# Adaptive products kept out of the first seam of a two-layer decoder trunk, and the openings behind the other seams in three passes over half a PSUM bank

## The chip, the cores and the metric

The kernel runs on one core of one Trainium2 chip. The metric is the device time of one execution in microseconds (us); the profile is one further execution with the hardware profiler on.

## What is computed

Two layers on 256 tokens of width 2048, batch 1, in float32. In both, every sub-layer is a root-mean-square norm, a shift and a scale that depend on a condition vector `c`, the sub-layer, and a residual add with a gate that depends on `c` too.

```python
cond = silu(c)
for i in range(2):
    sh1, sc1, g1, sh2, sc2, g2 = split(cond @ ada_w[i] + ada_b[i], 6)   # the adaptive columns
    h = rmsnorm(x, norm_mix[i]) * (1 + sc1) + sh1
    y = attn_pool_mixer(h) if i == 0 else ssd_mixer(h)
    x = x + g1 * y
    h = rmsnorm(x, norm_ffn[i]) * (1 + sc2) + sh2
    x = x + g2 * (square(relu(h @ ffn_w1[i])) @ ffn_w2[i])              # hidden width 8192
return rmsnorm(x, final_norm)
```

The mixer of layer 0 is windowed attention in three head groups beside a pooling branch; that of layer 1 is a chunked state-space scan (Mamba-2).

## The kernel before, in words

**GEMMs.** Tokens and weights are split into a high part in the `fp32r` format and a low part, the remainder, so a product takes three terms: high by high, high by low, low by high. `split` (lines 163 to 168) makes the parts of a weight tile: ScalarE copies the high part (166), VectorE subtracts (167). Weight tiles `raw` of 1 MB come through SP's DMA queue into a ring of four; each is split in two halves into rings of four `hi` and four `lo` tiles. An activation tile `h(kt)` has 512 columns: 256 tokens high, then 256 low. `mm` (194 to 203) forms the terms in one of two ways. With `one` it makes three passes of 256 columns that all add into half a PSUM bank. Otherwise the first pass streams high and low tokens together, 512 columns, and the second adds the low weight into the second half of the bank; the two halves are joined later by `evac` (303 to 306): a ScalarE copy and a VectorE add. Each pass has a weight load of its own. Tiles that go through `mm` with `one` start 64 bytes after an aligned address (`SHIFT`).

**Adaptive columns.** Each of 192 jobs (`ada_tile`, 83 to 87) loads a 1 MB tile of `ada_w` into the same `raw` ring, multiplies it with the condition on VectorE and sums along the row (line 86). `Feed.tick`, called after each weight load, runs jobs at an even rate: `Feed(jobs, slots)` spreads them over so many loads. The 36 jobs that mixer 0 gets are the first gate and 20 of the 32 that the norm before the first MLP needs; the other 12 run in `up_wide` (474 to 494), one per k-tile.

**Seams.** Where one sub-layer ends and the next begins, the residual is gated (`gated`, lines 445 and 446), squared and summed (315), the root is taken on GpSimd (337), the row is scaled (370, 372), turned on TensorE (393) and modulated. At the first seam (mixer 0 to MLP 0) `turn_out` copies the turned blocks to `xr`: blocks 0 and 2 on VectorE (403), 1 and 3 on ScalarE (401). `up_wide` then makes `h` from them (408 to 416) and runs a GEMM over all of PSUM with row tiles `w1w`. At the other two seams, into mixer 1 and into MLP 1, `opening` runs the first GEMM (three output tiles beside the 64 time-step columns, and four output tiles). For k-tiles 0 to 7 it goes over the first 128 tokens, then over the other 128 (`mm_chunk`, lines 209 and 210), while the rest of the input is still being turned; for k-tiles 8 to 15 it takes both at once (245, 246). Its weights come from a `Stream`.

**Order.** The Tile framework plans the order of each engine's instructions when the kernel is built, by priorities and a model of their costs; on the chip each engine runs its list in that order, and so does SP's DMA queue.

Of the kernel before, what the change touches and what calls it, by code (L numbers as in the profile page):

```python
# [8 lines left out]
F32 = mybir.dt.float32  # L9
F32R = mybir.dt.float32r  # L10
AF = mybir.ActivationFunctionType
# [27 lines left out]
def trunk(ctx, tc, xin, cb, fin, adaT, par, m0, m1, tri_in, icnt, pw_in,  # L39
# [130 lines left out]
    class Stream:  # L170
# [5 lines left out]
        def half(self, i):  # L176
            while len(self.halves) <= i:
                n = len(self.halves)
                ap, nk = self.aps[n // 2]
                if n % 2 == 0:  # L180
                    self.raw = wp.tile([P, D], F32, name="raw")
                    SP.dma_start(self.raw[:, 0:nk * self.width], ap)
                size = nk // 2 * self.width
                self.halves.append(split(wp, self.raw[:, (n % 2) * size:(n % 2 + 1) * size], nk // 2))
                if n % 2:
                    feed[0].tick()
            return self.halves[i]
# [16 lines left out]

    def mm_chunk(acc, hi, lo, r, c, first, last):

        def part(ap):
            return ap.rearrange("p (s c t) -> p s c t", s=2, c=2)[:, :, c, :]
        PE.matmul(part(acc), hi, part(r), start=first and c == 0, stop=False, skip_group_check=True)
        PE.matmul(acc[:, T + c * P:T + (c + 1) * P], lo, r[:, c * P:(c + 1) * P], start=False, stop=last, skip_group_check=True)  # L210

    def opening(h, stream, nt, extra=None):


        acc = [accp.tile([P, 512], F32, name="acc") for _ in range(nt)]

        def tiles(kt):
            hi, lo, n = stream.half(kt // 2)
            for t in range(nt):
                ts = slice(t * P, (t + 1) * P)  # L220
                yield acc[t], hi[:, kt % 2, ts], lo[:, kt % 2, ts], h(kt)

        for kt in range(8):
            if kt == 2:
                h.piece_of(1, 0)
            if kt == 6:
                h.piece_of(0, 1)
            for a, hi, lo, r in tiles(kt):
                mm_chunk(a, hi, lo, r, 0, kt == 0, False)
        if extra:  # L230
            extra = extra()
        for kt in range(8):
            if kt == 1:
                h.piece_of(1, 1)
            if kt in (2, 4, 6):
                stream.half(3 + kt // 2)
            if kt in (2, 6):
                h.piece(2 + kt // 4)
            for a, hi, lo, r in tiles(kt):
                mm_chunk(a, hi, lo, r, 1, False, False)  # L240
            if extra:
                extra(kt)
        for kt in range(8, KT):
            for a, hi, lo, r in tiles(kt):
                PE.matmul(a, hi, r, start=False, stop=False, skip_group_check=True)
                PE.matmul(a[:, T:2 * T], lo, r[:, 0:T], start=False, stop=(kt == KT - 1), skip_group_check=True)
            if extra:
                extra(kt)
        return acc
# [49 lines left out]

    def chunks(ap, n=4):  # L300
        return [(ap[c], n) for c in range(ap.shape[0])]

    def evac(ps, dst, parts=P):
        corr = tp.tile([P, T], F32, name="corr", bufs=1)
        S.activation(corr[0:parts], ps[0:parts, T:2 * T], AF.Copy)
        V.tensor_tensor(dst, ps[0:parts, 0:T], corr[0:parts], op=ALU.add)


    ssq = [None, None]
# [30 lines left out]
    class Hidden:  # L340
# [55 lines left out]
        def turn_out(self, i, c):  # L396
            ps = self.turned_of(i, c, i % 2 == 0)
            dst = self.xr[:, i * 4:(i + 1) * 4, c * P:(c + 1) * P]
            src = ps.rearrange("p (k t) -> p k t", k=4)
            if i % 2:  # L400
                S.activation(dst, src, AF.Copy)
            else:
                V.tensor_copy(dst, src)

        def affine(self, kt):
            return mod[self.l][self.a][:, kt:kt + 1], mod[self.l][self.b][:, kt:kt + 1]
# [67 lines left out]
    def up_wide(h, jobs):  # L474
# [5 lines left out]
        with tc.tile_pool(name="sweep1", bufs=4) as fp:  # L480
            acc = [accp.tile([P, 512], F32, name="acc") for _ in range(5)] + [misc.tile([P, 512], F32, name="mp") for _ in range(3)]
            for kt in range(KT):
                for half in range(2):
                    if half == 0:
                        h.make(kt, h.xr[:, kt, :])
                    elif jobs:
                        ada_run(jobs.pop(0))
                    hi, lo, _ = load_row(w1w[kt, :, half * 1024:(half + 1) * 1024], fp)
                    for j in range(8):
                        n = half * 8 + j  # L490
# [5 lines left out]
    def mlp(l, h, nx, wide=()):  # L496
# [3 lines left out]
        with tc.tile_pool(name=f"mlp{l}", bufs=2) as mp:  # L500
# [7 lines left out]
            def new_z():  # L508
                return mp.tile([P, T], F32, name="z", bufs=3)
# [8 lines left out]
            def up(q, b, first=False):  # L518
                acc = opening(h, h.stream, 4) if first else gemm_ws(chunks(w1[l, q * 4 + b]), h, 512, one=True)
                ht = new_hid(q, b)  # L520
                for t in range(4):
                    z = new_z()
                    if first:
                        evac(acc[t], z)
                    squared_relu(z if first else acc[t], z, ht, t)

            def down(q, b):
                def done(acc, c):
# [50 lines left out]
    def mixer0(ctx0, jobs2, following):  # L579
# [54 lines left out]
        with tc.tile_pool(name="mix0", bufs=2) as mp:  # L634
# [64 lines left out]
                S.activation(cat_a[sl, pr, 0:T], o[sl, 0:T], AF.Copy)  # L699
                V.tensor_tensor(cat_a[sl, pr, T:2 * T], o[sl, 0:T], cat_a[sl, pr, 0:T].bitcast(F32), op=ALU.subtract)  # L700

            feed[0] = Feed(jobs2, 31)
            tiles = []
            for b in range(6):
                if b:
# [65 lines left out]
    def mixer1(h, nx):  # L771
        with tc.tile_pool(name="mix1", bufs=2) as mp:
# [54 lines left out]
            def conv_silu(ps, ch, dst):  # L827
                xp = mp.tile([P, 3 + T], F32, name="xp")
                G.memset(xp[:, 0:3], 0.0)
                if ps.shape[1] == T:  # L830
                    S.activation(xp[:, 3:], ps, AF.Copy)
                else:
                    evac(ps, xp[:, 3:])
                cv = mp.tile([P, T], F32, name="cv")
                S.activation(cv, xp[:, 0:T], AF.Identity, bias=pcol(C_CB + ch), scale=pcol(C_CW + ch))
                for j in range(1, 4):
# [271 lines left out]
```

## Time and profile before

| | |
|---|---|
| median of three executions | 2560.23 us (2559.2 to 2566.05) |
| the profiled execution | 2565.11 us, span 2563.3 us from the first to the last instruction |
| TensorE passes | 2480.7 us busy, 97%, 15752 passes |
| weight loads on TensorE | 2217.8 us busy, 87% |
| VectorE | 1855.4 us busy, 72% |
| ScalarE | 1301.8 us busy, 51% |
| adaptive products (line 86) | 192, 2288 ns each |
| transfers | 664 MB, 259 GB/s on average |

TensorE's share is so high that a stage is read by where TensorE waits, for whom, and at which clock it runs. A pass is a MATMUL row, PE in the views; a weight load is a LDWEIGHTS row, PEld. VectorE is DVE, ScalarE ACT, GpSimd POOL, and SPq is SP's DMA queue. Durations of passes overlap, since they are pipelined: the pace is read from start to start.

### The profile page before, as it was taken

How to read it: one execution, taken by the hardware profiler on the slowest of the kernel's cores; microseconds unless marked ns; L12 is line 12 of the kernel's file. 1: busy time of each engine (PE TensorE's matmuls, PEld its weight loads, DVE VectorE, ACT ScalarE, POOL GpSimd, SP SyncE). 2: the span in 40 equal slices, each digit the busy share in tenths (PEclk: the TensorE clock that was granted, in tenths of full speed). 3: DMA queues.
4: the chain of work that ended last, by engine and by line, in shares of the span. 5: the costliest groups of instructions: out<-in, count | busy, mean ns of one | idle time of the engine just before them, and what ended most of it. 6: DMA issues, size and time to landing. Idle time of an engine off the chain costs nothing.

```text
span 2563.3 us, 39160 instructions
## 1 busy us (share of the span) xinstructions
PE 2480.7 (97%) x15752; PEld 2217.8 (87%) x15752; DVE 1855.4 (72%) x2432; ACT 1301.8 (51%) x1927; POOL 18.1 (1%) x76
## 2 busy tenths in 40 slices
PE   6899989999999999999999999999999999999998
PEld 5589879989889899888888878888898998998996
DVE  7977798667777886778887888776776655456555
ACT  4355546644435445457664654664554453453453
POOL 0000000000000000000000000000000000000000
PEclk9999999999999999999999999999999999999999
DMA  9988898688887887746677777655567765555553
GB/s 392 417 341 311 299 334 291 249 305 325 309 327 292 299 316 293 268 165 233 242 276 255 244 258 251 205 187 185 191 249 277 265 245 197 185 193 192 186 189 124
DMA packets 117830, 664.02 MB, mean 259 GB/s; under 512 B 11664, under 2 KB 28432, under 8 KB 49424
## 3 DMA queue, kind: packets, MB, share of 16 engines
q1 hardware_dynamic: 117440, 661.42, 71.2%
q8 instruction: 123, 2.02, 0.3%
q14 instruction: 59, 0.48, 0.1%
q10 hardware_dynamic: 208, 0.10, 0.0%
HBM read 659.28 MB, written 2.20 MB: 258 GB/s over the span
## 4 chain that ended last, share of the span: by engine, by line
PE 82%; DVE 8%; DMA 5%; ACT 2%; issue 2%; POOL 0%; SPq 0%; ACTq 0%; DVEq 0%; POOLq 0%
PE acc L275 13%; PE acc L276 13%; PE acc L274 13%; PE acc L200 12%; PE acc L198 12%; PE acc L199 12%; DMA raw<-in_adaT_dram 5%; DVE lo L167 3%; DVE raw L86 2%; PE mp L903 1%; DVE cv L837 1%; ACT hi L166 1%; PE mp L697 0%; PE mp L393 0%; PE mp L199 0%
## 5 line engine op out<-in xcount | busy, mean ns | idle before, releaser
L166 ACT ACTIVATE hi<-raw 128x1024 fp32r<-128x1024 f32 (+1 forms) x800 | 818.5, 1026 | 962.1 <-PE acc L276 539.5
L167 DVE TENSOR_TENSOR lo<-raw,hi 128x1024 fp32r<-128x1024 f32 (+1 forms) x800 | 935.6, 1179 | 490.3 <-ACT hi L166 487.6
L200 PE MATMUL acc<-h,lo 128*128 128x256 f32 x2992 | 836.4, 281 | 7.3 <-DVE lo L167 7.1
L198 PE MATMUL acc<-h,hi 128*128 128x256 f32 x2992 | 839.1, 281 | 1.4 <-DVE dt_v L783 0.8
L199 PE MATMUL acc<-h,hi 128*128 128x256 f32 x2992 | 839.3, 281 | 0.0
L199 PEld LDWEIGHTS acc<-h,hi 128*128 128x128 f32 x2992 | 569.7, 190 | 2.2 <-issue 1.7
L200 PEld LDWEIGHTS acc<-h,lo 128*128 128x128 f32 x2992 | 561.3, 188 | 10.9 <-DVE lo L167 9.2
L198 PEld LDWEIGHTS acc<-h,hi 128*128 128x128 f32 x2992 | 564.2, 189 | 6.9 <-issue 4.3
L86 DVE SCALAR_TENSOR_TENSOR raw<-raw,cond 128x2048 f32<-128x2048 f32 x192 | 439.2, 2288 | 99.7 <-DMA raw<-in_adaT_dram 99.3
L274 PE MATMUL acc<-hi,hid 128*128 128x512 f32 x1024 | 398.6, 389 | 0.0
L275 PE MATMUL acc<-lo,hid 128*128 128x512 f32 x1024 | 398.4, 389 | 0.0
L276 PE MATMUL acc<-hi,hid 128*128 128x512 f32 x1024 | 398.3, 389 | 0.0
L274 PEld LDWEIGHTS acc<-hi,hid 128*128 128x128 f32 x1024 | 192.2, 188 | 39.9
L276 PEld LDWEIGHTS acc<-hi,hid 128*128 128x128 f32 x1024 | 192.2, 188 | 39.9
L275 PEld LDWEIGHTS acc<-lo,hid 128*128 128x128 f32 x1024 | 192.2, 188 | 39.5
L275 PE MATMUL acc<-lo,h 128*128 128x512 f32 x288 | 114.4, 397 | 2.3 <-DVE lo L167 2.3
L276 PE MATMUL acc<-hi,h 128*128 128x512 f32 x288 | 116.5, 405 | 0.0
L274 PE MATMUL acc<-hi,h 128*128 128x512 f32 x288 | 113.9, 397 | 0.3 <-ACT hi L166 0.3
L166 ACT ACTIVATE hi<-rawh 128x1024 fp32r<-128x1024 f32 x64 | 60.7, 949 | 97.2 <-DMA rawh<-in_wvq_dram 60.5
L275 PE MATMUL acc<-lo,yn 128*128 128x512 f32 x224 | 87.6, 391 | 0.0
L274 PE MATMUL acc<-hi,yn 128*128 128x512 f32 x224 | 87.5, 391 | 0.0
L276 PE MATMUL acc<-hi,yn 128*128 128x512 f32 x224 | 87.4, 390 | 0.0
(230 smaller groups left out, 2342.3 us busy)
## 6 DMA issues: line engine op xcount, KB each, us to landing
raw<-in_w_dram SPq DMA_DIRECT2D x240, 1024.0 KB, 5.0
raw<-in_adaT_dram SPq DMA_DIRECT2D x192, 1024.0 KB, 6.6
raw<-in_sx_dram SPq DMA_DIRECT2D x64, 768.0 KB, 4.3
raw<-in_sz_dram SPq DMA_DIRECT2D x32, 1024.0 KB, 5.0
raw<-in_swo_dram SPq DMA_DIRECT2D x32, 1024.0 KB, 4.9
raw<-in_wqk_dram SPq DMA_DIRECT2D x20, 1024.0 KB, 6.9
rawh<-in_wvq_dram SPq DMA_DIRECT2D x32, 512.0 KB, 12.2
rawh<-in_w1w_dram SPq DMA_DIRECT2D x32, 512.0 KB, 6.3
```

The costliest lines, as they stand in the source:

```text
L86: V.scalar_tensor_tensor(raw, raw, 1.0, cond, op0=ALU.mult, op1=ALU.mult, accum_out=acc_ada[l][:, i * KT + kt:i * KT + kt + 1])
L166: S.activation(hi, src, AF.Copy)
L167: V.tensor_tensor(lo, src, hi.bitcast(F32), op=ALU.subtract)
L198: PE.matmul(acc, hi, r[:, 0:T], start=first, stop=False, skip_group_check=skip)
L199: PE.matmul(acc, hi, r[:, T:2 * T], start=False, stop=False, skip_group_check=skip)
L200: PE.matmul(acc, lo, r[:, 0:T], start=False, stop=last, skip_group_check=skip)
L274: PE.matmul(acc[c], ah, hi, start=first, stop=False)
L275: PE.matmul(acc[c], ah, lo, start=False, stop=False)
L276: PE.matmul(acc[c], al, hi, start=False, stop=last)
L837: V.scalar_tensor_tensor(cv, xp[:, j:j + T], pcol(C_CW + j * 48 + ch), cv, op0=ALU.mult, op1=ALU.add)
L903: PE.matmul(ps[:, i * 64:(i + 1) * 64], em[c][:, i, :], xdt[c][:, i * 64:(i + 1) * 64], start=True, stop=True)
```

## The change

Four edits. The feed of mixer 0 spreads its 36 jobs over 26 weight loads in place of 31. `turn_out` remembers its last VectorE copy, and the twelve products in `up_wide` are put behind that copy on VectorE (`issue_after` adds an order of issue for the instructions on that copy's engine, and no wait for another engine). `mm_chunk` and the second part of `opening` make three passes into half a bank, where they made two over the whole; the streamed weight tiles start 64 bytes further on. So `evac` goes, and its users read PSUM directly. The time-step columns keep their two passes and their whole bank.

```diff
@@ class Stream, half
-                self.halves.append(split(wp, self.raw[:, (n % 2) * size:(n % 2 + 1) * size], nk // 2))
+                self.halves.append(split(wp, self.raw[:, (n % 2) * size:(n % 2 + 1) * size], nk // 2, SHIFT))
@@ mm_chunk
-        def part(ap):
-            return ap.rearrange("p (s c t) -> p s c t", s=2, c=2)[:, :, c, :]
-        PE.matmul(part(acc), hi, part(r), start=first and c == 0, stop=False, skip_group_check=True)
-        PE.matmul(acc[:, T + c * P:T + (c + 1) * P], lo, r[:, c * P:(c + 1) * P], start=False, stop=last, skip_group_check=True)
+        rh, rl = r[:, c * P:(c + 1) * P], r[:, T + c * P:T + (c + 1) * P]
+        out = acc[:, c * P:(c + 1) * P]
+        PE.matmul(out, hi, rh, start=first and c == 0, stop=False, skip_group_check=True)
+        PE.matmul(out, hi, rl, start=False, stop=False, skip_group_check=True)
+        PE.matmul(out, lo, rh, start=False, stop=last, skip_group_check=True)
@@ opening
-        acc = [accp.tile([P, 512], F32, name="acc") for _ in range(nt)]
+        acc = [accp.tile([P, 512], F32, name="acc")[:, 0:T] for _ in range(nt)]
...
-                PE.matmul(a, hi, r, start=False, stop=False, skip_group_check=True)
-                PE.matmul(a[:, T:2 * T], lo, r[:, 0:T], start=False, stop=(kt == KT - 1), skip_group_check=True)
+                mm(a, hi, lo, r, False, kt == KT - 1, True, True)
@@ evac
-    def evac(ps, dst, parts=P):
-        corr = tp.tile([P, T], F32, name="corr", bufs=1)
-        S.activation(corr[0:parts], ps[0:parts, T:2 * T], AF.Copy)
-        V.tensor_tensor(dst, ps[0:parts, 0:T], corr[0:parts], op=ALU.add)
@@ turn_out
-                V.tensor_copy(dst, src)
+                self.turned_last = V.tensor_copy(dst, src)
@@ up_wide
-                        ada_run(jobs.pop(0))
+                        with tc.issue_after(h.turned_last.ins):
+                            ada_run(jobs.pop(0))
@@ mlp, up
-                    z = new_z()
-                    if first:
-                        evac(acc[t], z)
-                    squared_relu(z if first else acc[t], z, ht, t)
+                    squared_relu(acc[t], new_z(), ht, t)
@@ mixer0
-            feed[0] = Feed(jobs2, 31)
+            feed[0] = Feed(jobs2, 26)
@@ mixer1, conv_silu
-                if ps.shape[1] == T:
-                    S.activation(xp[:, 3:], ps, AF.Copy)
-                else:
-                    evac(ps, xp[:, 3:])
+                S.activation(xp[:, 3:], ps, AF.Copy)
```

## Rows read from the trace of the kernel before

**Rows 1.** Stretches: start:end, length; busy PE, PEld, DVE, ACT, POOL; clock; DMA; GB/s

```profile
141.00:340.00 199.00, 196.52 (x1481) 178.30 (x1480) 157.69 (x238) 107.74 (x174) 0.25 (x4) 0.99 0.84 312
352.00:372.00 20.00, 17.35 (x77) 13.78 (x75) 19.96 (x30) 8.90 (x15) 0.00 (x0) 1.00 0.94 354
372.00:395.00 23.00, 13.93 (x55) 11.57 (x55) 20.96 (x35) 11.42 (x19) 1.27 (x2) 0.65 0.91 343
395.00:480.00 85.00, 85.00 (x721) 85.00 (x720) 63.18 (x79) 45.65 (x60) 0.00 (x0) 1.00 0.80 286
```

**Rows 2.** TensorE's passes in order of time at the first seam; start, length (us)

```profile
372.29 0.79 PE L275 MATMUL acc<-lo,cat_p 128*128 128x512 f32 x1 [2.93 <-DVE lo L167]
...
378.34 0.39 PE L275 MATMUL acc<-lo,cat_p 128*128 128x512 f32 x1
378.57 0.39 PE L276 MATMUL acc<-hi,cat_p 128*128 128x512 f32 x1
385.29 1.12 PE L393 MATMUL mp<-ident,xr 128*128 128x128 f32 x4 [6.34 <-ACT xr L370]
...
394.98 1.18 PE L198 MATMUL acc<-h,hi 128*128 128x256 f32 x5
```

**Rows 3.** VectorE in order of time there: products of line 86, last copy

```profile
367.12 2.29 DVE L86 SCALAR_TENSOR_TENSOR raw<-raw,cond 128x2048 f32<-128x2048 f32 x1
...
374.49 2.28 DVE L86 SCALAR_TENSOR_TENSOR raw<-raw,cond 128x2048 f32<-128x2048 f32 x1
...
387.91 2.28 DVE L86 SCALAR_TENSOR_TENSOR raw<-raw,cond 128x2048 f32<-128x2048 f32 x1
...
394.51 0.69 DVE L403 COPY xr<-mp 128x512 f32<-128x512 f32 x1 [1.47 <-PE mp L393]
```

**Rows 4.** Loads (PEld) and passes (PE) of the opening of MLP 1

```profile
1835.27 0.19 PEld L209 LDWEIGHTS acc<-h,hi 128*128 128x128 f32 x1
1835.32 0.33 PE L209 MATMUL acc<-h,hi 128*128 128x256 f32 x1
...
1835.49 0.22 PE L210 MATMUL acc<-h,lo 128*128 128x128 f32 x1
...
1835.55 0.33 PE L209 MATMUL acc<-h,hi 128*128 128x256 f32 x1
...
1836.65 0.19 PEld L209 LDWEIGHTS acc<-h,hi 128*128 128x128 f32 x1
```

**Rows 5.** Loads of the opening of mixer 1 at the half clock

```profile
1112.87 0.33 PEld L210 LDWEIGHTS acc<-h,lo 128*128 128x128 f32 x1
...
1113.72 0.33 PEld L210 LDWEIGHTS acc<-h,lo 128*128 128x128 f32 x1
```

**Rows 6.** Loads of a GEMM in three passes of 256 columns, in MLP 0

```profile
600.02 0.19 PEld L200 LDWEIGHTS acc<-h,lo 128*128 128x128 f32 x1
...
601.44 0.19 PEld L200 LDWEIGHTS acc<-h,lo 128*128 128x128 f32 x1
```

**Rows 7.** The chain of waits: 64-column passes of mixer 1, start, length

```profile
1184.15 3.52 PE mp L903 x32
```

**Rows 8.** SP's DMA queue in the attention stage; weight loads and job loads

```profile
251.31 0.33 SPq L157 DMA_DIRECT2D raw<-in_wqk_dram  x1
...
256.63 0.33 SPq L157 DMA_DIRECT2D raw<-in_wqk_dram  x1
258.84 6.51 SPq L85 DMA_DIRECT2D raw<-in_adaT_dram  x2
267.35 0.33 SPq L157 DMA_DIRECT2D raw<-in_wqk_dram  x1
```

**Rows 9.** Busy time by stretch, the two openings; columns as in rows 1

```profile
1109.80:1129.60 19.80, 18.60 (x137) 17.11 (x138) 19.07 (x48) 11.78 (x31) 0.60 (x3) 0.91 0.52 176
1835.00:1856.10 21.10, 19.33 (x152) 19.07 (x153) 20.17 (x48) 12.84 (x29) 0.62 (x1) 0.92 0.42 145
```

**Rows 10.** TensorE's waits behind the opening of mixer 1: us, times, longest

```profile
PE acc L198 <- DVE dt_v L783: 0.8, 1, 0.8
```

## The prediction

> **What bounds the kernel now.** I read the stretches first. From 141 to 340 us, the attention stage, TensorE is busy 196.5 of 199 us while VectorE is busy 158 [rows 1]: passes set the pace and the VectorE work lies under them. In the next two stretches, the end of the output projection and the seam to the MLP, this turns round: VectorE is busy 19.96 of 20 us and 20.96 of 23, and TensorE idles 2.65 and 9.07 us, 11.7 together, at a granted clock of 0.65 in the second [rows 1]. After 395 us the wide first GEMM has TensorE busy without a gap and VectorE 63 of 85 us [rows 1].
>
> Then TensorE's order of time in that seam. At 372.29 it had waited 2.93 us for the low half of a weight tile (line 167); the next 23 starts take 6.28 us, 0.27 each, where the last two are 0.23 apart; from the last, 378.57, to the first pass of the MLP, 394.98, are 16.4 us, most of it waits for the scaled and turned input [rows 2]. VectorE's order says what stood in front: the adaptive products of line 86, 2.2 to 2.3 us each. One starts at 367.12, just before the late low half; three more start from 374.49 to 387.91, and the copy out of PSUM that ends the turning comes at 394.51 [rows 3].
>
> Last the two openings (mixer 1 and MLP 1). In the first chunks each k-tile and output tile take a weight load and a pass for the high part, then both for the low part. The loads follow each other evenly: from 1835.27 to 1836.65 there are 12 steps, 0.115 us each, whether the pass beside them has 256 or 128 columns [rows 4]. At the half clock it is the same even step, 0.85 us for 4, 0.21 each [rows 5]. Where each load has a pass of 256 columns the step is 1.42 us for 12, 0.118 [rows 6]. Even 32 passes of only 64 columns, each with its load, need 3.52 us, 0.110 each [rows 7]. So a pass with a load of 128 columns costs about 0.115 us however few columns it streams, and the chunk passes are bound by loads, two per step, 0.230.
>
> **The first part: products moved out of the seam.** The feed of 36 jobs ends after 26 loads in place of 31, so 36 x 26/31 = 30 are out by load 26 now and six more must go into the attention stage. Of the twelve jobs of the wide GEMM three run in front of the last turned copy now [rows 3]; all twelve are to run behind it.
> (a) The late low half: the two products in front of it are gone. 2.9 us of wait, and 23 x (0.27 - 0.23) = 1.0 us of half clock behind the wait [rows 2]: 3.9.
> (b) Three products that stand in VectorE's queue on the way to 394.51, 2.2 us each from start to start: 6.6 [rows 3].
> (c) Against it, the MLP's first passes now start just as the clock comes back (0.65 in that stretch [rows 1]); earlier they may run some us at the half clock. A short stretch of it cost 1.0 in (a); I take 1.0.
> Seam: 3.9 + 6.6 - 1.0 = 9.5 gained. Bounds: 5, if other VectorE work (splits of the first weights, gating) slides into the freed places; 14, all 11.7 us of idle and what the half clock costs the passes and turnings of the second stretch, some 2.3 more.
> (d) The six jobs that move: 6 x 2.2 = 13 us of VectorE under passes that leave it 41 us free [rows 1], and 6 MB more through SP's queue and the four-slot ring of raw tiles that weights and jobs share. That ring is the cost. Two weight loads with one job between them are issued 5.3 us apart (251.31, 256.63); with two jobs between them the next comes 10.7 us later (267.35) [rows 8]. Ten of 26 loads get two jobs instead of four. The splits run some tiles ahead, and head work of attention lies between the GEMMs, so most of it is hidden; without this cover six such gaps are 6 x 5.4 = 32 us. I take 1.0, with 0 and 6 as ends, since TensorE shows no loss where the pattern occurs now.
> (e) The held products meet a GEMM with 22 us of VectorE to spare [rows 1]; SP issues their transfers in order and a fifth waits for the first product, with the next rows of weights behind it, but several k-tiles are split or loaded by then. 0; if the cover fails, the 6.6 of (b) come back.
>
> **The second part: three passes over half a bank.** Each of the 16 chunks (8 k-tiles, 2 halves of the tokens) of 3 + 4 output tiles goes from two loads and passes to three: 112 times 0.345 in place of 0.230, that is 112 x 0.115 = 12.9 us more on TensorE. For the k-tiles 8 to 15 the columns stay 768, each load beside 256 of them, 0.118 each [rows 6]: 0, at most 0.5. The shift of the streamed tiles by 64 bytes changes no instruction count: 0. Cover: TensorE idles 1.20 and 1.77 us in the two stretches, VectorE being busy nearly throughout [rows 9]; longer passes fill these 3.0. The granted clock there is 0.91 and 0.92 [rows 9], some 3.5 us lost; with fewer waits I let a third of it go, 1.2. So 12.9 - 3.0 - 1.2 = 8.7 lost. Bounds: 6.4 (all of the half clock gone) to 13.4 (nothing covered).
> The copies and adds that joined the two halves of a bank go: they lie beside passes, but the next GEMM waited 0.8 us for the last accumulator to come free after the opening of mixer 1 [rows 10]. 0.8 gained; bounds 0 (that wait belongs to the time-step columns, which keep their bank) and 1.
>
> The Trainium skill, "TensorE: Matmul & The Clock Gate", section Back-to-back issue gap, speaks of about 81 ns per pass in a stream of load and pass pairs at 128 columns. By it three passes are 0.243 against 0.230 and this part costs 112 x 0.013 = 1.5 us; no row here shows a pair under 0.110.
>
> **Sum.** -9.5 + 1.0 + 8.7 - 0.8 = -0.6 us on the profiled execution's 2565.1 (span 2563.3), which lies 4.9 us above the median of the three runs, 2560.23. On that median 2559.6: no change. About 0.3%, 7.7 us, is what a measurement of this kernel tells from none.
>
> **Rivals.** *All of the seam comes back* (0.12). All 11.7 us of idle vanish, attention hides the moved jobs, and the openings come to their lower bound because their waits and the half clock go: -14 + 6.4 - 1.0 = -8.6, 2551.6. For it: VectorE alone fills that seam. Against it: gating, squares, the power on GpSimd, scaling and turning remain a chain without any product.
>
> *Short passes are not bound by loads* (0.06). In the opening the 256-column pass lies 0.17 us before the next and the 128-column one 0.06 [rows 4]; read so, the strided pass is slow and three plain ones cost 0.174: 112 x 0.056 = 6.3 gained, half of it in front of waits, so -9.5 + 1.0 - 3.1 - 0.8 = -12.4, 2547.8. The even load steps and rows 7 speak against it. By 0.243 a triple it is -9.5 + 1.0 + 1.5 - 0.8 = -7.8, 2552.4; that is the time by the skill's section named above.
>
> *The clock falls in the chunk passes* (0.12), the one that ends slower. A chunk pass will stream 128 columns beside each load, where two loads have 384 now; in the two openings the clock has already been down for part of the time [rows 9], each time after waits and turning. At the half clock a triple costs 0.64 [rows 5] in place of 0.345. It decides from (7.7 + 0.6)/0.30 = 28 of the 112 triples on; with 60 of them at half clock +18 - 0.6, 2577. For it: streams with transposes between. Against it: the 64-column block of rows 7 ran at its full step.
>
> *The ring starves attention* (0.05): (d) beyond its end, above 9.3 us of the 32; at 12, 2570.6.
>
> *The products stay in the seam* (0.05), since the planner of the order places them by its own clock: only (a) comes, -3.9 + 1.0 + 8.7 - 0.8 = +5.0, 2565.2, no change by the bound.
>
> **How the numbers follow.** The forecast has 0.60. Within 0.3%: 0.60 + 0.05 = 0.65. Faster: 0.12 + 0.06 = 0.18. Slower: 0.12 + 0.05 = 0.17. The range takes the bounds of (a) to (d) and of the second part against each other, which seldom all fall on one side: 2551 to 2568; it leaves out the stronger half of each tail.
>
> **What would show it.** In the profile after: no line 86 between about 335 us and the last copy of line 403; the wait of 2.9 us gone; the first MLP pass 9 to 10 us earlier relative to the end of the attention stage, and that stage not over 1 us longer. In the openings three loads per step, evenly 0.115 us apart, and each opening 3 to 5 us longer. I am wrong if the loads follow at less than 0.1 us, if the clock in the openings falls under 0.85, or if the attention stage grows by more than 6 us.

## The result, and the profile after

The changed kernel takes 2577.69 us in the median (four executions, 2577.35 to 2581.04), the kernel before 2563.11 beside it (2559.2 to 2566.05): 14.6 us more, a ratio of 1.0061 with a 95% interval of 1.0041 to 1.0080. A second comparison on another chip gave 1.0053 (1.0037 to 1.0070). So it is slower by about 0.55%; the forecast was no change, and the range ended at 2568. The profiled execution took 2577.81 us, span 2576.0.

Its stretches, with the columns of [rows 1] (attention, the pooling stage and start of the projection, the first seam, the chunk passes of the openings of mixer 1 and MLP 1):

```profile
141.00:340.00 199.00, 194.05 (x1458) 174.95 (x1457) 157.47 (x238) 101.78 (x168) 0.25 (x4) 0.99 0.83 316
340.00:360.00 20.00, 14.73 (x57) 11.10 (x56) 18.35 (x33) 7.65 (x10) 0.00 (x0) 0.91 0.91 350
372.00:395.00 23.00, 18.56 (x82) 14.88 (x81) 15.38 (x23) 11.39 (x19) 1.28 (x2) 0.89 0.61 213
1112.90:1142.90 30.00, 29.73 (x185) 28.33 (x184) 23.12 (x54) 14.10 (x33) 0.69 (x3) 0.72 0.39 135
1847.70:1871.90 24.20, 24.18 (x217) 24.02 (x216) 21.66 (x51) 13.54 (x30) 0.62 (x1) 1.00 0.36 128
```

Attention left TensorE 2.5 us idle in [rows 1]; here it is 5.0. A gap of 5.3 us between 340 and 360 is new; there the kernel before had

```profile
340.00:360.00 20.00, 20.00 (x88) 16.18 (x87) 19.20 (x32) 8.23 (x14) 0.00 (x0) 1.00 0.88 306
```

The two chunk stretches, 19.8 and 21.1 us in [rows 9], are 30.0 and 24.2, and in the first the granted clock is 0.72. TensorE in order of time from the projection to the wide GEMM, as in [rows 2]:

```profile
340.97 0.50 PE L275 MATMUL acc<-lo,cat_a 128*128 128x512 f32 x1 [0.22 <-DVE lo L167]
...
352.34 1.16 PE L727 MATMUL mp<-dif,pw 128*128 128x256 f32 x2 [5.05 <-DVE dif L725]
...
386.96 0.39 PE L276 MATMUL acc<-hi,cat_p 128*128 128x512 f32 x1
389.77 0.96 PE L388 MATMUL mp<-ident,xr 128*128 128x128 f32 x4 [2.42 <-ACT xr L365]
392.75 4.96 PE L388 MATMUL mp<-ident,xr 128*128 128x128 f32 x24 [2.02 <-DVE xr L367]
...
398.38 0.85 PE L198 MATMUL acc<-h,hi 128*128 128x256 f32 x5
...
401.04 0.39 PE L199 MATMUL acc<-h,hi 128*128 128x256 f32 x1 [1.29 <-DVE h L410]
```

The wait of 2.93 us for the late low half is gone, and from the last projection pass to the first MLP pass are 11.4 us, not 16.4. But the projection ends at 386.96, not 378.57: among other things a wait of 5.05 us for the last pooled difference has come up inside it. VectorE says what stood there, and what follows the last turned copy:

```profile
345.35 2.28 DVE L86 SCALAR_TENSOR_TENSOR raw<-raw,cond 128x2048 f32<-128x2048 f32 x1
...
348.36 2.28 DVE L86 SCALAR_TENSOR_TENSOR raw<-raw,cond 128x2048 f32<-128x2048 f32 x1
...
352.11 0.18 DVE L725 TENSOR_TENSOR dif<-fix,win 128x16 f32<-128x16 f32 x1
...
397.75 0.69 DVE L398 COPY xr<-mp 128x512 f32<-128x512 f32 x1
398.36 2.28 DVE L86 SCALAR_TENSOR_TENSOR raw<-raw,cond 128x2048 f32<-128x2048 f32 x1
400.57 0.08 DVE L86 DVE_READ_ACCUMULATOR raw<-raw,cond 128x1 f32 x1
400.57 0.42 DVE L410 TENSOR_TENSOR h<-hf,h 128x256 fp32r<-128x256 f32 x1
```

No product lies between 350.6 and 398.4, as the change wants; the first one behind the copy stands in front of the first low half of `h` (line 410), which is the 1.29 us above. SP's queue shows where the projection's loads went: the first is issued at 320.03, in the kernel before at 304.04.

```profile
311.88 6.15 SPq L85 DMA_DIRECT2D raw<-in_adaT_dram  x2
320.03 0.33 SPq L157 DMA_DIRECT2D raw<-in_wo_dram  x1
```

Weight loads in the two openings, mixer 1 first:

```profile
1114.83 0.19 PEld L210 LDWEIGHTS acc<-h,hi 128*128 128x128 f32 x1
1114.94 0.19 PEld L211 LDWEIGHTS acc<-h,lo 128*128 128x128 f32 x1
1115.05 0.19 PEld L209 LDWEIGHTS acc<-h,hi 128*128 128x128 f32 x1
...
1115.68 0.19 PEld L209 LDWEIGHTS acc<-h,hi 128*128 128x128 f32 x1 [0.21 <-ACT h L431]
1116.21 0.19 PEld L210 LDWEIGHTS acc<-h,hi 128*128 128x128 f32 x1 [0.35 <-DVE h L432]
...
1118.02 0.33 PEld L210 LDWEIGHTS acc<-h,hi 128*128 128x128 f32 x1
1118.23 0.33 PEld L211 LDWEIGHTS acc<-h,lo 128*128 128x128 f32 x1
1118.44 0.33 PEld L209 LDWEIGHTS acc<-h,hi 128*128 128x128 f32 x1
1118.65 0.33 PEld L210 LDWEIGHTS acc<-h,hi 128*128 128x128 f32 x1
...
1850.19 0.19 PEld L211 LDWEIGHTS acc<-h,lo 128*128 128x128 f32 x1
1850.30 0.19 PEld L209 LDWEIGHTS acc<-h,hi 128*128 128x128 f32 x1
...
1851.41 0.19 PEld L210 LDWEIGHTS acc<-h,hi 128*128 128x128 f32 x1
```

Three even loads a step, 0.111 us each (1850.30 to 1851.41 are ten). In mixer 1 the granted clock went to its lower level, 1.2 GHz, at 1117.0, behind transposes and two waits of 0.21 and 0.35 us, and stayed there for 17.1 us: 0.21 us a load, 0.63 a step (1118.02 to 1118.65). In MLP 1 no wait breaks the chunk passes, and the granted clock stays at 2.4 GHz (1.00 in the stretch above).

### The profile page after: what moved, and what is told of

It reads as the page before. It is cut to its first block, busy times and chain, and to the rows that moved or that the text cites. A ratio compares the mean times of both kernels' runs of the same rounds, so it can differ in the third digit from the quotient of the medians.

```text
span 2576.0 us, 39484 instructions
## 1 busy us (share of the span) xinstructions
PE 2491.7 (97%) x15920; PEld 2229.5 (87%) x15920; DVE 1852.6 (72%) x2425; ACT 1304.1 (51%) x1925; POOL 23.2 (1%) x76
## 4 chain that ended last, share of the span: by engine, by line
PE 80%; DVE 7%; DMA 7%; ACT 3%; issue 2%; POOL 0%; SPq 0%; ACTq 0%; DVEq 0%; POOLq 0%
PE acc L276 12%; PE acc L275 12%; PE acc L274 12%; PE acc L200 12%; PE acc L199 12%; PE acc L198 12%; DMA raw<-in_adaT_dram 6%; DVE lo L167 2%; DVE raw L86 2%; ACT hi L166 1%; PE mp L894 1%; DVE cv L828 1%; PE acc L210 1%; DMA rawh<-in_w1w_dram 1%; PE acc L211 1%
## 5 line engine op out<-in xcount | busy, mean ns | idle before, releaser
L200 PE MATMUL acc<-h,lo 128*128 128x256 f32 x3048 | 849.2, 281 | 5.5 <-DVE lo L167 5.4
L199 PE MATMUL acc<-h,hi 128*128 128x256 f32 x3048 | 853.0, 281 | 1.3 <-DVE h L410 1.3
L198 PE MATMUL acc<-h,hi 128*128 128x256 f32 x3048 | 853.3, 281 | 0.8 <-ACT hi L166 0.8
L199 PEld LDWEIGHTS acc<-h,hi 128*128 128x128 f32 x3048 | 580.6, 191 | 4.3 <-issue 2.4
L198 PEld LDWEIGHTS acc<-h,hi 128*128 128x128 f32 x3048 | 575.3, 189 | 7.2 <-issue 3.7
L200 PEld LDWEIGHTS acc<-h,lo 128*128 128x128 f32 x3048 | 572.1, 189 | 9.8 <-DVE lo L167 7.5
L276 PE MATMUL acc<-hi,hid 128*128 128x512 f32 x1024 | 398.4, 389 | 0.0
```

The source lines that it names most:

```text
L198: PE.matmul(acc, hi, r[:, 0:T], start=first, stop=False, skip_group_check=skip)
L199: PE.matmul(acc, hi, r[:, T:2 * T], start=False, stop=False, skip_group_check=skip)
L200: PE.matmul(acc, lo, r[:, 0:T], start=False, stop=last, skip_group_check=skip)
L276: PE.matmul(acc[c], al, hi, start=False, stop=last)
```

## The experiments

Each ratio is to the kernel before on the same chip; it compares means, so it is not always the quotient of the two medians. 0.0010 is 2.6 us. The kernels with half products and half transfers, and the kernel before again, have a profile only. The second table is read from the traces. A: first projection load issued, first and last projection pass, and first pass of MLP 0, all in us after attention's first score pass. Seam: from the last projection pass to the first of MLP 0. Chunks: from first to last chunk pass of each opening, and the time of it at the lower clock level.

| kernel | median | before beside it | ratio | 95% interval |
|---|---|---|---|---|
| changed, again | 2579.65 | 2568.16 | 1.0053 | 1.0037 to 1.0070 |
| products alone (36 over 26, and hold) | 2568.57 | 2566.27 | 1.0009 | 0.9999 to 1.0018 |
| openings alone | 2573.24 | 2566.27 | 1.0025 | 1.0015 to 1.0035 |
| 36 over 26 alone | 2571.20 | 2566.27 | 1.0019 | 1.0010 to 1.0029 |
| hold alone | 2566.26 | 2566.27 | 0.9995 | 0.9985 to 1.0006 |
| products alone, pooling first | 2579.14 | 2568.16 | 1.0053 | 1.0035 to 1.0070 |
| opening of MLP 1 alone | 2569.89 | 2568.16 | 1.0013 | 0.9999 to 1.0026 |
| opening of mixer 1 alone | 2577.70 | 2565.74 | 1.0038 | 1.0024 to 1.0053 |
| third load in both openings | 2579.14 | 2567.36 | 1.0047 | 1.0032 to 1.0063 |
| changed, 36 over 31 | 2571.95 | 2567.36 | 1.0021 | 1.0010 to 1.0032 |
| two jobs moved, hold | 2562.00 | 2567.36 | 0.9982 | 0.9971 to 0.9994 |
| two jobs moved, products late | 2559.75 | 2567.36 | 0.9972 | 0.9962 to 0.9981 |
| the same with a short pass | 2566.36 | 2565.74 | 0.9999 | 0.9983 to 1.0014 |

```
kernel                      A: load  first  last   MLP 0  seam | chunks mixer 1, MLP 1 (lower clock)
before                        159.2  183.1  233.7  250.1  16.4 | 19.3 (3.4)   21.0 (3.4)
before, again                 160.8  185.1  235.8  252.0  16.2 | 18.9 (0)     21.0 (3.4)
changed                       174.3  188.5  241.3  252.7  11.4 | 29.9 (17.1)  24.1 (0)
changed, again                174.9  189.1  243.0  254.7  11.7 | 28.0 (6.8)   24.1 (0)
products alone                174.5  188.6  242.6  254.3  11.7 | 18.9 (0)     21.0 (3.4)
36 over 26 alone              176.2  190.3  243.4  256.9  13.6 | 18.9 (0)     21.0 (3.4)
hold alone                    158.7  183.0  233.5  247.0  13.5 | 18.9 (0)     19.4 (0)
pooling first                 176.8  191.0  245.3  257.0  11.7 | 18.9 (0)     21.0 (3.4)
changed, 36 over 31           159.2  183.5  235.5  247.4  11.9 | 28.0 (6.8)   24.1 (0)
two moved, hold               163.4  186.1  232.4  243.7  11.4 | 18.9 (0)     21.0 (3.4)
two moved, late               160.8  184.0  230.2  241.8  11.6 | 18.9 (0)     19.4 (0)
half products                 173.6  188.9  238.3  251.8  13.6 | 18.9 (0)     21.0 (3.4)
half transfers                164.7  189.9  235.6  254.2  18.6 | 19.3 (3.4)   21.0 (3.4)
openings alone                158.5  182.4  233.1  249.5  16.4 | 29.5 (10.2)  24.1 (0)
opening of MLP 1 alone        160.0  183.9  233.2  249.8  16.6 | 18.9 (0)     24.1 (0)
opening of mixer 1 alone      159.8  184.1  233.3  249.9  16.6 | 30.0 (17.1)  19.4 (0)
third load                    159.2  183.5  232.7  249.3  16.6 | 28.1 (6.8)   24.2 (0)
```

### The two parts, and the two halves of the first

The products alone are the first part of the diff without the rest; the openings alone the rest without the first part; then each half of the first part:

```diff
-            feed[0] = Feed(jobs2, 31)
+            feed[0] = Feed(jobs2, 26)
```

```diff
-                        ada_run(jobs.pop(0))
+                        with tc.issue_after(h.turned_last.ins):
+                            ada_run(jobs.pop(0))
```

> The kernel before with the first part alone: the 36 jobs over 26 loads, and the twelve products held behind the last turned copy. Theory A (from the trace after): the denser jobs make the weight loads and the pooling chain late, the last pass of the output projection comes 8.4 us later, the seam itself is 5.0 us shorter and the wide GEMM 1.6, so the first w2 pass comes about 1.8 us later; median 2 us above before, between 0 and +5. Prediction on record: 9.5 gained less 1.0, 8.5 below before. Rival B (the parts don't add, because each build gets an order of its own for the whole kernel): anything, and the change after the wide GEMM is as large as in front of it.

> The kernel before with the second part alone: three passes over half a bank in both openings, without the copies and adds behind them. Theory A: the opening of mixer 1 loses about 10 us (48 triples by 0.115 = 5.5, and the half clock over some 17 us), that of MLP 1 nothing once its waits are filled; median 9 to 13 us above before. Prediction on record: 8.7 lost less 0.8, 7.9 above. If the fall of the clock in the trace after hung on where the first part had left the order, the clock holds here and the median is 0 to 5 above.

> The kernel before with its 36 jobs over 26 loads in place of 31, and nothing else. Theory A: attention and output projection end about 8 us later, and the three products stay in the seam; median 4 to 8 above before. Prediction on record: the late low half goes, 3.9 gained, less 1.0: 2.9 below.

> The kernel before with the twelve products held behind the last turned copy, and nothing else; the 36 jobs stay over 31 loads. Theory A and the prediction on record agree: attention and the late low half stay as they are, three products of 2.2 us leave the seam, 5.6 to 6.6 gained, and the median is 4 to 7 below before. Rival: the chain of gate, square, power, scale and turn is as long without the products, and the median is within 2 us of before.

The products alone give +2.3 us by their ratio (-0.3 to 4.6), not the 8.5 gained that are on record; the openings +6.4 (3.8 to 9.0), where 7.9 were. 36 jobs over 26 loads give +4.9 (2.6 to 7.4) for a forecast of -2.9, and the hold -1.3 (-3.8 to 1.5) for -5.6. So it was the first part that failed most. For the hold the rival came, within 2 us of before; the openings alone lie between the two ranges of their expectation, and why is not known. In the second table the projection ends 7.6 us later with 26 loads (mean 242.3 of the changed kernel's two profiles and the products alone, to 234.7 of the two before), 4.6 of them in front of its first pass, and the seam is 4.7 shorter with both halves. The hold alone shortens it by 2.8, since another chain is left, as TensorE's order in that run shows:

```profile
381.52 0.66 PE L393 MATMUL mp<-ident,xr 128*128 128x128 f32 x4 [1.98 <-ACT xr L370]
385.16 2.82 PE L393 MATMUL mp<-ident,xr 128*128 128x128 f32 x12 [2.98 <-DVE xr L372]
389.28 3.68 PE L393 MATMUL mp<-ident,xr 128*128 128x128 f32 x16 [1.30 <-ACT xr L370]
392.60 0.94 PE L198 MATMUL acc<-h,hi 128*128 128x256 f32 x5
```

From the span's start the first turning comes 3.8 us earlier than in [rows 2], the first MLP pass only 2.4: the scaled rows of the second half of the tokens are late next.

### The kernels once more

Nothing is changed in these two; they give a second profile of each kernel and a comparison on the chip of the others.

> The changed kernel once more, beside runs of the kernel before on the same chip. If the parts add, it is 6.5 (openings alone) + 2.3 (products alone) = 8.8 above before; if they work on one another, for instance because the clock in the opening of mixer 1 stays down longer, some 14.6 as in the first comparison. In its profile: the two values of the three-pass step that the first traces show (0.340 and 0.353 us a triple) fall on the same stages as in the first profile if the program sets them, on others if each execution does.

> The kernel before once more, for a second profile. Theory: which of the two values a three-pass GEMM runs at (0.340 or 0.353 us a triple; 681 triples at the shorter and 2258 at the longer in the first profile) is chosen anew in each execution at the waits; then this profile has other counts, and spans of profiles differ by several us for that reason alone. Rival: the program sets it, and the counts are the same within some 50.

The changed kernel is 13.6 us slower by its ratio (9.5 to 18.0), where the parts alone make 8.7; the intervals touch, so whether the parts work on one another isn't settled here. The kernel before had 416 triples at the shorter step and 2173 at the longer behind 390 us in its first profile, 893 and 1672 in its second: the execution chooses, not the program (last section). Its second profile is 6.1 us longer in spite of it: TensorE waits 80.5 us in all in place of 72.3, 4.4 of it between 900 and 1060 us, and the granted clock is low for 3.1 us more. A single pair of profiles can't tell differences of this size. The second table, which takes short stretches, repeats within some 3 us: the projection's end lies at 232.7 to 235.8 in the eight traces that keep 36 jobs over 31 loads, and at 241.3 to 243.4 in the four with 26 loads, pooling first left aside.

### Pooling before the products

The products alone, with the jobs that the projection's loads start held behind the last pooled difference:

```diff
+        behind[0] = pooled.ins
         for b0 in (0, 2):
...
-        ada_tile(l, i, kt)
+        if behind[0] is None:
+            ada_tile(l, i, kt)
+        else:
+            with tc.issue_after(behind[0]):
+                ada_tile(l, i, kt)
```

> The products part alone (as in the run of that name), with the jobs that the output projection's loads start held behind the last step of the pooling chain on VectorE. Theory A: the wait of 5.1 us for the pooled difference behind two products and its 3.4 us of half clock go, and the output projection ends 4 to 6 us earlier than with the products part alone: 2 to 4 below before in the median. Rival (the ring of raw tiles makes the projection late): the held products keep their ring slots longer, the loads of the projection come later still, and the median is 0 to 6 above the products part alone.

My theory of the pooling chain falls: 1.0053, 11 us above the products alone by the two ratios, though the projection ends only 2.7 us later; where the rest is lost I didn't follow. The wait has only changed its name:

```profile
351.65 0.73 PE L280 MATMUL acc<-hi,cat_p 128*128 128x512 f32 x2 [1.32 <-ACT hi L172]
356.77 0.79 PE L281 MATMUL acc<-lo,cat_p 128*128 128x512 f32 x1 [4.39 <-DVE lo L173]
```

Three products now stand in one row in front of low halves whose tiles came late. The question is why the tiles are late.

### Transfers or products

36 jobs over 26 loads, with half of each product, or half of each transfer, left out (adaptive columns of mixer 0's jobs are then wrong):

```diff
-        V.scalar_tensor_tensor(raw, raw, 1.0, cond, op0=ALU.mult, op1=ALU.mult,
+        n = D // 2 if half[0] else D
+        V.scalar_tensor_tensor(raw[:, 0:n], raw[:, 0:n], 1.0, cond[:, 0:n], op0=ALU.mult, op1=ALU.mult,
```

```diff
+            SP.dma_start(raw[:, 0:D // 2], adaT[l, i * KT + kt][:, 0:D // 2])
+            for j in range(2):
+                V.scalar_tensor_tensor(raw[:, 0:D // 2], raw[:, 0:D // 2], 1.0, cond[:, j * 1024:(j + 1) * 1024], op0=ALU.mult, op1=ALU.mult,
```

> 36 jobs over 26 loads and nothing else of the change, and in these 36 jobs the product on VectorE takes only half of the row; the other half is left out, so the adaptive columns are wrong. The transfers stay whole. Read from the trace: the first load of the output projection after the start of attention (159 to 161 us over 31 loads, 174 to 176 over 26), and the projection's last pass (233.5 to 235.8 and 241.3 to 243.4). If the transfers and the ring make it late, 170 to 176 and 238 to 243 here; if the products on VectorE do, 156 to 164 and 231 to 236.

> 36 jobs over 26 loads and nothing else of the change, and these 36 jobs load only half of their rows; the product is made of two over that half, so VectorE is as busy as before and the adaptive columns are wrong. If the transfers and the ring make the projection's loads late, the first comes 156 to 165 us after the start of attention and the projection's last pass at 231 to 237; if the products on VectorE do, 170 to 176 and 238 to 243.

With half products the first projection load is as late as with whole ones (173.6 to 176.2) and the projection ends at 238.3, 5.1 earlier; with half transfers the load comes at 164.7 and the end at 235.6, 7.8 earlier. So the transfers and the ring that they share with the weights make that load late, not the time of the products. But what both runs take away lies in the projection alone. Its stretch from first to last pass with whole jobs, half products and half transfers:

```profile
338.20:391.60 53.40, 48.13 (x202) 38.44 (x200) 48.05 (x77) 23.82 (x36) 0.55 (x1) 0.94 0.83 315
335.50:385.30 49.80, 46.70 (x200) 36.67 (x198) 45.21 (x75) 24.49 (x36) 0.55 (x1) 1.00 0.87 337
335.70:381.80 46.10, 46.05 (x202) 37.03 (x200) 41.70 (x68) 22.41 (x32) 0.00 (x0) 1.00 0.90 336
```

TensorE idles 5.3, 3.1 and 0 us in it. The projection's first pass is late in all three: 190.3, 188.9 and 189.9, where the kernel before has 183.1 and 185.1. The part of the delay that arises in attention goes with neither half, and its cause stays open. With half transfers the seam is 18.6, with three products in it where the run with whole jobs has one, and at the first MLP pass only 2.7 of the 7.8 are left.

By the traces 27 whole jobs are issued in front of the projection's first load in the kernel before and 33 in the changed one. The six, 6.3 million bytes, are 20 us at the 316 GB/s of the stretch above, an estimate, and the load is 15.1 later. Bytes alone don't set it: with half transfers 17.3 million bytes of jobs are in front of it, in the kernel before 28.3, and it still comes 4 to 5 us later than before.

### The same end without denser jobs

Two jobs more go to the wide GEMM and the 34 that are left over 29 loads, so that the last loads carry none, as with 26; in the second run the products are also held behind the input of their own k-tile:

```diff
-    early = 20
+    early = 18
-            feed[0] = Feed(jobs2, 31)
+            feed[0] = Feed(jobs2, 29)
...
-                    elif jobs:
+                    elif jobs and kt:
+                        with tc.issue_after(h.made.ins):
```

> The kernel before with the twelve products held behind the last turned copy, two more jobs sent from mixer 0 to the wide GEMM (34 and 14 in place of 36 and 12), and the 34 spread over 29 loads: 1.17 jobs per load, as in the kernel before (1.16), where the change has 1.38. Theory A (the denser jobs are what the first part costs, and the late low half is cured by any version whose last two loads carry no job): attention and projection end no later than before, the wait of 3.0 us for the low half goes, 3 us of the seam come from the hold; median 3 to 6 below before. Rival (the product that stood in front of the low half only hands its place to other work): 0 to 2 below, as with the hold alone.

> As the run with two jobs moved, but each of the fourteen products stands behind the finished input of its own k-tile of the wide GEMM, from the second k-tile on, so that none is in front of the first input. Theory: the first passes of the wide GEMM waited 1.8 to 2.4 us behind one product where it was held only behind the turned copy; 1 to 2 us below the run with two jobs moved. Rival: the wide GEMM waits for its first low halves anyway, and the two agree within 1 us.

0.9982 and 0.9972: 4.6 and 7.2 us (4.9 to 9.8) gained. The projection ends 3.4 us earlier than before in the mean, the seam is 11.5 us, and in the second run the first MLP pass comes 9.3 us earlier than in the mean of the two profiles before. TensorE there:

```profile
378.45 0.66 PE L393 MATMUL mp<-ident,xr 128*128 128x128 f32 x4 [2.42 <-ACT xr L370]
381.35 5.75 PE L393 MATMUL mp<-ident,xr 128*128 128x128 f32 x28 [2.24 <-DVE xr L372]
387.20 0.85 PE L198 MATMUL acc<-h,hi 128*128 128x256 f32 x5
```

The second version beats both kernels, and its projection takes 46.2 us from first to last pass, with hardly a wait, where the kernel before takes 50.7. The two runs' intervals overlap, so what the later place of the products brings is not settled.

### The openings

Three passes in one opening alone (`one` is true where there are four output tiles, or three), and then the kernel before with a third load and pass of 128 columns a step in its whole bank, which counts the low weight twice:

```diff
+        one = nt == 4
         acc = [accp.tile([P, 512], F32, name="acc") for _ in range(nt)]
+        if one:
+            acc = [x[:, 0:T] for x in acc]
```

```diff
         PE.matmul(acc[:, T + c * P:T + (c + 1) * P], lo, r[:, c * P:(c + 1) * P], start=False, stop=False, skip_group_check=True)
+        PE.matmul(acc[:, T + c * P:T + (c + 1) * P], lo, r[:, c * P:(c + 1) * P], start=False, stop=last, skip_group_check=True)
```

> The kernel before with three passes over half a bank in the opening of MLP 1 alone; mixer 1's opening keeps two passes and its copies and adds. Theory A: 64 triples by 0.112 = 7.2 less the 1.8 of waits and the 1.7 of half clock that stood there: 2 to 4 above before. Rival: the whole loss of the openings lies in mixer 1, where the clock falls, and this is within 1 us of before. Prediction on record: 64/112 of 7.9, 4.5 above.

> The kernel before with three passes over half a bank in the opening of mixer 1 alone. If the parts add: 6.5 less 3.3, 3.2 above before, though its opening gets 9 to 11 us longer in the trace with 7 to 17 us of half clock; then the scan behind it gives 5 to 7 back. If the trace is right and the medians of the two openings together were low: 7 to 10 above.

> The kernel before with a third load and pass of 128 columns in each chunk step of both openings, into the same whole bank: it repeats the product with the low weight, which is so counted twice for eight k-tiles. Copies and adds stay. It has the third load of the change, and more columns beside its loads. Theory A (the third load costs 0.112 us a step, 12.5 in all; the half clock of 10 to 17 us in the opening of mixer 1 comes on top in the change): 5 to 9 above before, and the granted clock in the two openings 0.9 or more. Prediction on record, without the copies: 8.7 above. Rival (a third pass with a load in the chunks always brings the clock down): a half clock of 10 us or more here too, 9 to 13 above.

MLP 1 alone gives +3.3 (-0.3 to 6.7), mixer 1 alone +9.8 (6.2 to 13.6), which is what the traces show and more than the two together in the first run. The third load and its pass alone, with the whole bank and the copies kept, are +12.1 (8.2 to 16.2), over the 5 to 9 that I expected, and the two stretches, 28.1 and 24.2 us from first to last pass, are those of the changed kernel's second profile within 0.1:

```profile
1114.90:1143.10 28.20, 24.84 (x182) 23.55 (x183) 22.40 (x53) 13.11 (x32) 0.57 (x2) 0.88 0.40 146
1843.50:1867.80 24.30, 24.25 (x216) 24.25 (x216) 21.83 (x51) 12.63 (x29) 0.62 (x1) 1.00 0.37 134
```

The cost lies in the third load with its pass, not in the half bank. In all six profiles with a third load in mixer 1 its opening is at the lower clock for 6.8 to 17.1 us; in the others in the table for 0 or 3.4. My expectation of a granted clock of 0.9 or more there was wrong by a little (0.88). Why the stay is so uneven, and whether the waits between the transposes or the shorter passes bring the clock down, no run here tells apart.

> The changed kernel with its 36 jobs back over 31 loads: the hold and the openings, without the denser jobs. If the parts add: -1.2 and +6.5, 5.3 above before. If the two parts of the change work on one another (13.6 above before in the second comparison, where the parts alone make 8.8): more than 7 above.

With the jobs back over 31 loads (the feed's diff above, undone in the changed kernel) the ratio is 1.0021, +5.4 us (2.6 to 8.2): hold and openings add as they stand alone (-1.3 and +6.4), and 36 over 26 accounts for the other 8 in the changed kernel, where it gave 4.9 alone.

### A short pass against the longer step

In the version with the products late, a short pass in each GEMM of three passes with four output tiles, 27 in the two MLPs and 6 in mixer 0, overwritten by the next. Its weight load has 16 columns, and it streams 128:

```diff
                     ts = slice(t * P, (t + 1) * P)
+                    if one and nt == 4 and k == 0 and t == 1:
+                        PE.transpose(acc[1][0:KT, 0:P], ident[:, 0:KT], ident)
```

> The version with two jobs moved and the products late, and with one short transposing pass of 16 columns, written over by the next pass, after the first product of each first GEMM of the MLPs that follows a second GEMM. If a short pass resets the step of a three-pass GEMM as the traces suggest (26 of 26 such passes on the slower step: half went to the faster), some half of 27 GEMMs of 64 triples gain 0.0134 us a triple, 11.6, less 27 passes of 0.14: 6 to 10 below the same version without it, 12 to 18 below before. If the step is set by something else: 2 to 5 above that version.

The triples get shorter as expected: 1497 at the shorter step behind 390 us in place of 507, 13.3 us at 0.0134 each. But the short pass does not send half of the GEMMs to the shorter step, as I had put it; it swaps the step: of 21 GEMMs that ran at one step right before it, 20 ran at the other behind it, 12 of 12 from the shorter to the longer and 8 of 9 the other way. The time doesn't fall: 0.9999, 7 us above the version without it by the two ratios, where I had 6 to 10 below. In the two profiles the 33 short passes cost some 0.12 us each, 4.0; TensorE waits 79.9 us in all in place of 70.7; and the granted clock is low for 7.1 us more, 3.6 lost. Together 16.8 against 13.3, and the span is 2.8 longer: most of what TensorE gains in these GEMMs comes back as waits.

## Why the prediction was wrong

**Step (d), the six moved jobs, failed.** I priced the pattern (32 us without cover), then took 1.0, with 6 as the far end, since TensorE showed no loss where two jobs in a row occur now. With 26 loads the projection ends at 242.3, in the two versions that keep the density at 231.3: 11.0 us in place of 1.0. Of these 3.7 lie in front of its first pass and 7.3 in the projection itself, where TensorE waits 5.3 us and then runs some us at the lower clock. That is the rival *the ring starves attention*, at the size that I wrote beside it (12) and gave 0.05, though more of it falls on the projection than on attention. That tiles split ahead hide one such gap and not six in a row is how I read it; the runs show the first projection load 15 us later and the waits in the projection gone with half transfers, not what makes attention late. The second mistake in (d) is its cover: 41 us of free VectorE are a mean over 199 us, while between 340 and 360 VectorE was busy 19.2 of 20 us in the kernel before already, with pooling, products and splits in one queue, so lateness there came out on TensorE at once.

**Steps (a) and (b).** (a) was right: 231.3 to 234.7 is 3.4 gained, 3.9 forecast (with the mean of all eight traces that keep 36 over 31, 233.9, it is 2.6). (b) was too large: 2.8 to 4.7 from the seam, 6.6 forecast. Three products of 2.2 us were in the queue, but not each was on the path; the second token half's chain and the first splits of the wide GEMM fill part of their places, as the lower bound of 5 for the seam had it. The seam's sum, 9.5, is reached by the version with the products late (9.3) and lies in its bounds; in the changed kernel (d) eats it: 11.0 - 3.4 - 4.7 = +2.9 at the first MLP pass, 2.65 in the traces (253.7, the mean of two, to 251.05) and 2.3 in the median of the products alone.

**Step (e)** failed in small: the first held product stands in front of the first low half of `h`, 1.3 us.

**The second part.** That a pass with its load takes about 0.115 us however few columns it streams was right (0.111), so was the triple at the lower clock (0.63 for 0.64). By the Trainium skill, "TensorE: Matmul & The Clock Gate", section Back-to-back issue gap, a pass of 128 columns in a stream of load and pass pairs takes about 81 ns, and by an estimate from it this part would have cost 1.5 us; the traces with three loads show 111 ns. Each opening was to grow by 3 to 5 us: MLP 1 does, by 3.1 (from 21.0, where part was at the lower clock) or 4.7 (from 19.4), so the cover of 3.0 and the 1.2 of clock were fair there. Mixer 1 grows by 8.7 to 11.1. There 48 steps by 0.111 are 5.3, and 6.8 to 17.1 us at the lower clock another 3.4 to 8.6, less what hides in waits: the rival *the clock falls in the chunk passes* came about in one opening of two. In the longest case some 21 steps of the 112 are at the lower clock, fewer than the 28 from which I had it decide, but it makes the openings dearer than the 7.9 forecast. How much dearer isn't settled: openings alone 6.4, the two apart 3.3 + 9.8 = 13.1, changed less products alone 11.3, changed with 31 loads less hold 6.7, the third load with copies kept 12.1. That this rival's 2577 is nearly the measured 2577.69 is luck: it needs 60 triples at the lower clock, and most of the loss has another cause.

**The sum.** On record -0.6; by what was measured +2.3 for the first part and 6.4 to 13.1 for the second, 8.7 to 15.4, where the changed kernel is at 13.6. Ten of that are step (d) going by the traces; by the times 36 over 26 is +4.9 alone and 8 in the changed kernel.

**The listed signs** held for the products and the late low half, and turned against me where they were to: attention with the projection grew by 7.6 us, over the 6 that I had named, and the clock in mixer 1's opening was 0.72, under 0.85. The first MLP pass was 4.7 us nearer to the projection's end, not 9 to 10.

## What to carry to other kernels

Price a moved transfer by its place in the queue, not by how one such gap looks now: count how many more stand in front of the first load of the next stage. Here six of 1 MB made that load 15 us late; bytes over rate gave 20, an estimate and no rule, as the run with half transfers shows. Free time of an engine is read in the 20 us where the moved work will land. Work taken out of a seam should go past the first input of the next stage, and from a dense stage to one with room: two jobs less in front were worth more than six jobs squeezed together.

## What the runs showed of the hardware that was not expected

A GEMM in three passes of 256 columns runs at one of two steps, with the same loads, tiles and clock level: 0.1178 us a pass in the kernel before at 430 us, 0.1133 in the changed one, 0.353 and 0.340 a triple. Here both, the kernel before first:

```profile
430.03 0.28 PE L198 MATMUL acc<-h,hi 128*128 128x256 f32 x1
...
431.09 0.28 PE L198 MATMUL acc<-h,hi 128*128 128x256 f32 x1
```

```profile
429.73 0.28 PE L200 MATMUL acc<-h,lo 128*128 128x256 f32 x1
...
431.09 0.28 PE L200 MATMUL mp<-h,lo 128*128 128x256 f32 x1
```

Nine steps take 1.06 us in the first, twelve 1.36 in the second. A GEMM keeps its step until something breaks the row of passes, a wait or a foreign pass, and then may take the other. In the 17 traces without the short pass 216 such GEMMs begin directly behind a pass of 512 columns with three triples in a row, and all begin on the longer step; the short pass above swapped the step in 20 of 21. The choice differs between executions of one program: the 477 triples between the two profiles of the kernel before are worth 6.4 us at 0.0134 each, which has to be kept in mind before a few us between two profiles are explained. In the run with the short pass such a gain did not show in the time.
